# A seven-product (Strassen) step for the second FFN matrix of an encoder kernel

## The chip, the cores and the metric

The kernel runs on one core of one Trainium2 chip. The metric is device time of one execution in microseconds (us), taken as the median of several executions; beside it stands one execution that the hardware profiler recorded. The engines are TensorE (PE in the profile, its weight loads PEld), VectorE (DVE), ScalarE (ACT), GpSimd (POOL) and SyncE (SP), which here only issues DMAs. Every engine takes its own list of instructions in order; an instruction whose operand is not there holds back all that stand behind it.

## The reference

Two layers, each with a mixing block and a SwiGLU block. What matters here is the SwiGLU block (S = 1024 rows, D = 1024, D_FF = 2816, all float32):

```python
h = _rmsnorm(x, g_pre_ffn[l])
gate, up = jnp.split(h @ w_ffn_in[l], 2, axis=-1)
f = (jax.nn.silu(gate) * up) @ w_ffn_out[l]
x = x + _rmsnorm(f, g_post_ffn[l])
```

`act = silu(gate) * up` is a matrix of 2816 x 1024 as the kernel holds it (columns of D_FF on the partitions, rows of the sequence along them), and the second product is `act.T @ w_ffn_out`.

## The kernel before

**Precision.** float32 operands are split into a high part of the faster fp32r format and a low part, what is left of it (`split`, lines 149 to 152: ScalarE casts the high part, VectorE or GpSimd subtracts it, lines 151 and 152). A product of two split matrices takes three matmuls, high by high, high by low and low by high.

**w_ffn_in.** `ffn_in` goes over 11 pairs of 128-column blocks. For each pair two `Quad`s (gate and up) do a seven-product step: sums of blocks of the weights (L1069) and of h (`Blocks`), seven products of 12 matmuls of 128x512 each (L1079), and sums that give the four blocks of the result, s2, z, y and s1 (`snap`, L1084; L1099 to L1115). `gate_out` applies silu, `up_out` multiplies (L1130) and writes two rows of blocks of act to DRAM (`actd`, L1134).

**w_ffn_out.** `ffn_out(l, actd, t0, n, out)` is called three times in a layer, for 3, 3 and 2 tiles of 128 rows. Each call goes over all 22 blocks ff of D_FF: `load_act` reads a block of act for its tiles, `load_ffn_out` the whole block of 128x1024 weights, both are split, and each tile takes 2 halves of the 1024 columns by 3 matmuls (L1179), into two PSUM banks per tile. The last two blocks are done tile by tile (`late = 2`), and `out` gets a tile when it is complete, copied from PSUM by ScalarE and VectorE (L1192, L1193).

**What `out` does.** `last_tile` loads the tile of x (L1306) into one of two slots (`xs_`). In layer 1 `residual_out` squares the tile (L310), computes the scale on GpSimd (L208, L210), multiplies it by scale and gain (L314), adds it to x (L315; GpSimd for tiles 1, 3 and 5) and stores two halves, one from SP and one from ScalarE's queue (L316). In layer 0 `residual` and `norm_x` do the same (L322 to L325) and the first norm of layer 1 (L284, L289), and `norm_T` transposes the tile (L301, target hTp) for layer 1's first matmuls (`zf`, target zT; `kvz`, target kvp).

**What sets the order.** The program is written in the order of the Python code, and a scheduler then places the instructions of each engine; the order within an engine is fixed before the kernel runs. Buffers are slots of two arenas, handed out by rings (`Ring`, `run(first, count, step)`); a slot is taken again when its last reader is done. Four more buffers of 8 KB a partition are called `big`. PSUM tags (`pd`, `av`, `sc`, `pT`) have two banks each. In layer 0 `mem.make()`, keys and values of the memory for layer 1 (targets mTp, kmp, vmp), stands ahead of the first `ffn_out`, and `zf_load` and `fourier_tables` stand between the second and the third.

Of the kernel before, what the change touches and what calls it, by code (L numbers as in the profile page):

```python
# [68 lines left out]
def tile_encoder(ctx: ExitStack, tc: tile.TileContext, T, C, out):  # L69
# [60 lines left out]
    qws, sns, silus, acts = Ring(32, 0, 16, 20), Ring(36, 38, 40, 42, 32, 34), run(8, 5, 2), run(18, 3, 4)  # L130
    sums, wsums = run(8, 4, 2), Ring(4, 6)
    wqs, ars, fs, xs_ = run(44, 3, 4), run(56, 2, 2), run(24, 3, 4), run(36, 2, 4)
# [3 lines left out]
    wcs, wos, ahs = Ring(112, 116, 96, 100, 48, 52, 56, 60), run(80, 6, 4), run(104, 3, 3)  # L136
# [255 lines left out]
    class Memory:  # L392
# [12 lines left out]

        def norm(self, mt):
# [3 lines left out]
            h = at(self.kx + 4 + 4 * mt, D)  # L410
            nc.sync.dma_start(h, T["mem"][0, mt * P : (mt + 1) * P, :])
# [27 lines left out]
        def make(self):  # L439
            self.load_k()  # L440
# [685 lines left out]
    def up_out(q, g, actd, p):  # L1126
        for i, c in enumerate(q.out):
            if i % 2 == 0:
                a = acts(S)
            (nc.gpsimd if i in (0, 3) else nc.vector).tensor_tensor(  # L1130
                out=a[:, 512 * (i % 2) : 512 * (i % 2) + 512], in0=c, in1=g[i], op=ALU.mult
            )
            if i % 2:
                nc.sync.dma_start(actd[2 * p + i // 2], a)  # L1134
# [20 lines left out]
    def load_ffn_out(l, ff):  # L1155
        hi, lo = wos(D, dt=F32R), wos(D, dt=F32R)
        raw = wqs(D)
        nc.sync.dma_start(raw, T["w_ffn_out"][l, ff * P : (ff + 1) * P])
        split(hi, lo, raw)
        return hi, lo  # L1160

    def load_act(actd, ff, t0, n):

        raw = ars(n * P)
        nc.sync.dma_start(raw, actd[ff, :, t0 * P : (t0 + n) * P])
        a = ahs(2, n * P, dt=F32R)
        split(a[:, 0], a[:, 1], raw)
        return a

    def ffn_out(l, actd, t0, n, out):  # L1170

        pts = [[ps([512], "fo", ("pd", "av", "sc")[t]) for _ in range(2)] for t in range(n)]

        def step(ff, t, a, w):
            sl = slice(t * P, t * P + P)
            for m in range(2):
                ns = slice(m * 512, m * 512 + 512)
                for j, (x, y) in enumerate(((0, 0), (0, 1), (1, 0))):
                    mm(pts[t][m], a[:, x, sl], w[y][:, ns], start=ff == 0 and j == 0, stop=ff == NFF - 1 and j == 2)  # L1179

        late = 2
        ops = {}
        for ff in range(NFF):
            ops[ff] = load_act(actd, ff, t0, n), load_ffn_out(l, ff)
            if ff < NFF - late:
                for t in range(n):
                    step(ff, t, *ops[ff])
        for t in range(n):
            for ff in range(NFF - late, NFF):
                step(ff, t, *ops[ff])  # L1190
            f = fs(D)
            nc.scalar.copy(f[:, 0:512], pts[t][0])  # L1192
            nc.vector.tensor_copy(f[:, 512:1024], pts[t][1])  # L1193
            out(t0 + t, f)
# [8 lines left out]
    actd = drp.tile([NFF, P, S], F32, name="actd")  # L1203
# [33 lines left out]
    for l in range(DEPTH):  # L1237
# [57 lines left out]
        if l + 1 < DEPTH:  # L1295
            mem = Memory(l + 1, 16, 0, 24, 36, "pT")
            mix = Mix(l + 1, nhT, mem)
            mem.make()

        def last_tile(t, f):  # L1300
# [9 lines left out]
            residual(x, f, st["gpf"])  # L1310
            st[t] = norm_x(x, st["gpn"], f)
            nc.sync.dma_start(x2d[t], x)
            if t:
                norm_T(st.pop(t - 1), nhT, t - 1, "pT")
# [53 lines left out]
```

## Time and profile before

| | |
|---|---|
| median of 3 executions | 2183.88 us (2183.79 to 2185.25) |
| the profiled execution's own time | 2182.96 us |
| span of its trace | 2181.2 us |
| busy: TensorE, VectorE, ScalarE, GpSimd | 95%, 68%, 50%, 29% |
| mean granted TensorE clock | 0.973 |
| read from HBM, written | 201.76 MB, 49.28 MB |
| w_ffn_out of layer 0, first matmul | at 845.0 us |
| w_ffn_out of layer 1, first matmul | at 1922.8 us |

The span runs from the first to the last recorded instruction. A row of the profile's timeline has the start in us, the length in us, the engine, the line of the kernel, the operation with target and source, and the count of instructions that are merged in it; in square brackets stand idle time ahead of it and what ended that. Rows of groups have busy time, mean time of one in ns, and idle time with what ended it. Busy times of TensorE overlap, since a matmul starts before the one ahead has ended.

### The profile page before, as it was taken

Reading aid. Unit: us, or ns where it says so; the run is one execution under the profiler, and the core shown is the slowest. Engines: PE = TensorE matmul, PEld = TensorE weight load, DVE = VectorE, ACT = ScalarE, POOL = GpSimd, SP = SyncE. Lnnn points to the kernel's source line nnn. Section 1 sums busy time; section 2 is a strip of 40 time slices with the busy share of each in tenths; the row PEclk is TensorE's granted clock in tenths of the full one; section 3 lists DMA queues with packets and bytes.
Section 4 is the critical chain, followed back from the end, with each engine's and each line's share of the span. In section 5 each row is a group of like instructions: output and inputs, shape, how many; then the busy total and the mean of one; then the engine's idle time right before and its main releaser. Section 6 shows DMA issues by size and latency. Waiting matters only on the chain.

```text
span 2181.2 us, 27953 instructions
## 1 busy us (share of the span) xinstructions
PE 2063.6 (95%) x9666; PEld 1708.7 (78%) x9666; DVE 1490.9 (68%) x2352; ACT 1083.4 (50%) x2221; POOL 626.0 (29%) x723
## 2 busy tenths in 40 slices
PE   6998998799999999999999979986999999999997
PEld 6886877588888887888888758775888888888876
DVE  7569767987777765464756686788877767644555
ACT  6467767553333334453545676675433333334343
POOL 4244436532222223010214334465222212100010
PEclk9999999799999999999999989997999999999999
DMA  7112223412223236565721122133222222255765
GB/s 224 37 49 63 73 83 116 135 62 84 87 68 97 78 100 228 195 229 179 239 86 51 35 73 103 53 127 105 74 91 78 97 78 81 92 188 169 245 206 179
DMA packets 135582, 252.87 MB, mean 116 GB/s; under 512 B 11256, under 2 KB 86032, under 8 KB 135440
## 3 DMA queue, kind: packets, MB, share of 16 engines
q1 hardware_dynamic: 127376, 232.20, 32.7%
q10 hardware_dynamic: 8064, 18.88, 2.2%
q8 instruction: 76, 1.25, 0.2%
q14 instruction: 66, 0.54, 0.1%
HBM read 201.76 MB, written 49.28 MB: 115 GB/s over the span
## 4 chain that ended last, share of the span: by engine, by line
PE 82%; DVE 7%; ACT 4%; DMA 3%; issue 2%; POOL 1%; SPq 0%; DVEq 0%; ACTq 0%; POOLq 0%
PE fo L1179 21%; PE qy L1079 11%; PE qz L1079 11%; PE qx L1079 11%; PE mo L162 7%; PE qw L1079 5%; PE qp L162 3%; PE kvp L162 3%; DVE arena_r L152 2%; PE av L767 2%; PE pT L760 2%; PE zT L162 1%; PE sc L723 1%; ACT arena_r L151 1%; DMA arena_f<-in_w_mem_kv 1%
## 5 line engine op out<-in xcount | busy, mean ns | idle before, releaser
L151 ACT CAST arena_r<-arena_f 128x512 fp32r<-128x512 f32 (+4 forms) x736 | 456.4, 640 | 749.3 <-PE fo L1179 170.2
L152 DVE TENSOR_TENSOR arena_r<-arena_f,arena_r 128x512 fp32r<-128x512 f32 (+3 forms) x632 | 515.0, 824 | 338.4 <-ACT arena_r L151 314.7
L1179 PE MATMUL fo<-arena_r 128*128 128x512 f32 x2112 | 490.5, 393 | 9.6 <-ACT arena_r L151 7.6
L1179 PEld LDWEIGHTS fo<-arena_r 128*128 128x128 f32 x2112 | 397.5, 189 | 95.0 <-ACT arena_r L151 9.3
L1079 PE MATMUL qy<-arena_r 128*128 128x512 f32 x1056 | 264.6, 400 | 26.9 <-ACT arena_r L151 24.9
L1079 PEld LDWEIGHTS qy<-arena_r 128*128 128x128 f32 x1056 | 203.3, 194 | 71.7 <-ACT arena_r L151 26.4
L1069 DVE TENSOR_TENSOR arena_f<-arena_f 128x512 f32<-128x512 f32 x220 | 222.2, 1013 | 12.4 <-DMA arena_f<-in_w_ffn_in 7.4
L1079 PE MATMUL qz<-arena_r 128*128 128x512 f32 x704 | 195.9, 389 | 0.0
L1099 POOL TENSOR_TENSOR arena_f<-arena_f 128x512 f32<-128x512 f32 x44 | 64.8, 1473 | 347.6 <-ACT arena_f L1084 347.6
L1079 PEld LDWEIGHTS qz<-arena_r 128*128 128x128 f32 x704 | 132.1, 188 | 27.7 <-DVE arena_r L152 0.3
L208 POOL TENSOR_SCALAR rrsv<-rss 128x1 f32<-128x1 f32 x32 | 11.9, 373 | 425.4 <-ACT arena_f L310 214.8
L1079 PE MATMUL qx<-arena_r 128*128 128x512 f32 x528 | 127.8, 389 | 0.0
L1079 PE MATMUL qw<-arena_r 128*128 128x512 f32 x528 | 127.5, 389 | 0.0
L152 POOL TENSOR_TENSOR arena_r<-arena_f,arena_r 128x256 fp32r<-128x256 f32 (+2 forms) x104 | 85.1, 824 | 146.9 <-ACT arena_r L151 129.1
L1079 PE MATMUL qx<-big,arena_r 128*128 128x512 f32 x528 | 127.1, 389 | 0.0
L1130 POOL TENSOR_TENSOR arena_f<-arena_f 128x512 f32<-128x512 f32 x44 | 72.0, 1636 | 188.9 <-DVE arena_f L1111 128.8
L1079 PE MATMUL qz<-big,arena_r 128*128 128x512 f32 x352 | 115.7, 389 | 0.0
L1079 PEld LDWEIGHTS qx<-arena_r 128*128 128x128 f32 x528 | 99.1, 188 | 20.5
L1079 PEld LDWEIGHTS qx<-big,arena_r 128*128 128x128 f32 x528 | 99.1, 188 | 20.5
L1079 PEld LDWEIGHTS qw<-arena_r 128*128 128x128 f32 x528 | 99.1, 188 | 20.5
L162 PE MATMUL mo<-arena_r 128*128 128x512 f32 x384 | 103.9, 414 | 5.0 <-ACT arena_r L151 4.6
L162 PE MATMUL mo<-big,arena_r 128*128 128x512 f32 x384 | 103.8, 409 | 2.7 <-ACT arena_r L151 1.4
(196 smaller groups left out, 3297.9 us busy)
## 6 DMA issues: line engine op xcount, KB each, us to landing
arena_f<-in_w_ffn_out SPq DMA_DIRECT2D x132, 512.0 KB, 3.6
arena_f<-in_w_ffn_in SPq DMA_DIRECT2D x88, 512.0 KB, 3.6
actd<-arena_f SPq DMA_DIRECT2D x44, 512.0 KB, 4.6
arena_f<-actd SPq DMA_DIRECT2D x88, 192.0 KB, 2.6
arena_f<-in_w_in SPq DMA_DIRECT2D x40, 256.0 KB, 2.9
arena_f<-in_x SPq DMA_DIRECT2D x16, 512.0 KB, 4.4
arena_f<-in_w_out SPq DMA_DIRECT2D x32, 256.0 KB, 2.6
pmd<-arena_f ACTq DMA_DIRECT2D x32, 256.0 KB, 2.0
```

Source lines behind the costliest of these rows:

```text
L151: nc.scalar.copy(hi, src)
L152: return (lo_eng or nc.vector).tensor_tensor(out=lo, in0=src, in1=f32(hi), op=ALU.subtract)
L162: mm(self.dst, a, b, start=self.i == 0, stop=self.i == self.n - 1)
L208: nc.gpsimd.tensor_scalar(out=v, in0=ss, scalar1=1.0 / n, scalar2=EPS, op0=ALU.mult, op1=ALU.add)
L723: mm(pt, lhs, self.kst[g][i][:, k0 * P : k1 * P], start=i == 0, stop=i == 1)
L760: nc.tensor.transpose(pT[:, h, :], es_[h // 2][:, h % 2, j * P : j * P + P], ident)
L767: mm(av, lhs, p_, start=j == 0 and i == 0, stop=j == nk - 1 and i == 1)
L1069: nc.vector.tensor_tensor(out=s, in0=a, in1=b, op=op)
L1079: mm(pt, a, b, start=start and n == 0, stop=n == 11, skip_group_check=not start)
L1099: nc.gpsimd.tensor_tensor(out=self.v, in0=self.v, in1=self.s2, op=ALU.add)
L1130: (nc.gpsimd if i in (0, 3) else nc.vector).tensor_tensor(out=a[:, 512 * (i % 2) : 512 * (i % 2) + 512], in0=c, in1=g[i], op=ALU.mult)
L1179: mm(pts[t][m], a[:, x, sl], w[y][:, ns], start=ff == 0 and j == 0, stop=ff == NFF - 1 and j == 2)
```

## The change

In `ffn_out` all 8 tiles of rows are taken at once as a 2 x 2 block scheme: act has blocks of 512 rows by the even or odd block of each pair in D_FF, the weights the same pairs by halves of the columns. Seven products i = 2, 4, 5, 3, 1, 7, 6 each go over 11 pairs k (a step): one operand of act (128x512) against one of the weights (128x512), for 4 tiles of 128 rows, by 3 matmuls. Products 4, 3 and 7 go on in the PSUM banks of 2, 5 and 1.

- `up_out` makes the seven operands of act in the w_ffn_in stage, three sums and two differences more per pair, on VectorE and GpSimd, and writes each to DRAM, in seven writes of 256 KB where there were two of 512 KB.
- `out_sums` loads one operand of act and one block of the weights (products 2 and 5) or two (the other five), adds or subtracts these (VectorE in even steps, GpSimd in odd ones), and splits both operands. Loads are of 256 KB.
- The sums of the products are kept in the four `big` buffers: copies by ScalarE, sums from PSUM by VectorE, and one difference by GpSimd (L1238) per tile.
- In layer 0 `mem.make()` comes behind product 2, `zf_load` and `fourier_tables` behind product 7; the rows of mem are loaded ahead of the memory's weights, in both layers. `residual` adds on GpSimd but for the last tile. Tiles 0 to 3 are put out within product 6, tiles 4 to 7 behind it.
- In layer 1 (`late`) product 6 is done tile by tile, and tiles 4 to 7 are put out one after the other. Finished operands have 15 slots in layer 1 and 6 in layer 0 (`abs_`), raw ones 3 for act (`ras`) and 6 for the weights (`rbs`).

```diff
-    wqs, ars, fs, xs_ = run(44, 3, 4), run(56, 2, 2), run(24, 3, 4), run(36, 2, 4)
+    ras, rbs, bsums, xs_ = run(40, 3, 2), run(46, 6, 2), Ring(58, 32, 34), Ring(36, 24)
...
     def up_out(q, g, actd, p):
+        V, G = nc.vector, nc.gpsimd
+        a = [acts(512) for _ in range(4)]
         for i, c in enumerate(q.out):
...
+            (G if i in (0, 3) else V).tensor_tensor(out=a[i], in0=c, in1=g[i], op=ALU.mult)
+        a11, a21, a12, a22 = a
...
+        put(3, a11)
+        put(4, a22)
+        for i, x, y, eng in ((1, a11, a22, G), (2, a21, a22, V), (5, a11, a12, G)):
+            s = acts(512)
+            eng.tensor_tensor(out=s, in0=x, in1=y, op=ALU.add)
+            put(i, s)
+        V.tensor_tensor(out=a21, in0=a21, in1=a11, op=ALU.subtract)
+        put(6, a21)
+        G.tensor_tensor(out=a12, in0=a12, in1=a22, op=ALU.subtract)
+        put(7, a12)
...
+    def out_sums(l, actd, i, k):
+        ab = abs_(2, 2, 512, dt=F32R)
+        raw = ras(512)
+        nc.sync.dma_start(raw, actd[i - 1, k])
+        split(ab[:, 0, 0], ab[:, 0, 1], raw)
...
+        if i in (2, 5):
+            s = block(i == 5, i == 5)
+        else:
...
+            x, y = block(*x), block(*y)
+            s = bsums(512)
+            (nc.vector, nc.gpsimd)[k % 2].tensor_tensor(out=s, in0=x, in1=y, op=op)
+        split(ab[:, 1, 0], ab[:, 1, 1], s)
+        return ab
...
+        for i in (2, 4, 5, 3, 1, 7, 6):
+            new = i in (2, 5, 1, 6)
+            if new:
+                pts = [ps([512], "fo", ("pd", "av", "sc", "pT")[p]) for p in range(4)]
+            ops = []
+            for k in range(n):
+                ops.append(out_sums(l, actd, i, k))
+                if i < 6 or i == 7 or not late:
+                    for p in range(4):
+                        step(pts[p], p, ops[k], k == 0, k == n - 1, new)
+                if i == 6 and k in (0, 2, 4, 6):
+                    t = (0, 2, 4, 6).index(k)
+                    out(t, fb[t][:, 0])
...
+                if i == 6 and late:
+                    out(4 + p, fb[p][:, 1])
+            after(i)
...
-            residual(x, f, st["gpf"])
+            residual(x, f, st["gpf"], nc.gpsimd if t < NT - 1 else None)
```

The scheduler's lists at three places, before and now.

SP at the entry of w_ffn_out in layer 0, before: loads of the weights of w_ffn_out, writes and reads of act, and the memory's weights.

```order
L339 DMA arena_f<-in_w_mem_kv 128x4x128 x3
L1158 DMA arena_f<-in_w_ffn_out 128x1024 x2
L339 DMA arena_f<-in_w_mem_kv 128x2x256
L339 DMA arena_f<-in_w_mem_kv 128x4x128
L339 DMA arena_f<-in_w_mem_kv 128x2x256 x2
L1158 DMA arena_f<-in_w_ffn_out 128x1024 x2
```

The same place now; the first read of act (L1178) is step 0's, the second step 1's, the third step 2's.

```order
L1178 DMA arena_f<-actd 128x512
L1140 DMA actd<-arena_f 128x512 x2
L1184 DMA arena_f<-in_w_ffn_out 128x512
L1140 DMA actd<-arena_f 128x512 x4
L339 DMA arena_f<-in_w_mem_kv 128x4x128
L1140 DMA actd<-arena_f 128x512
L339 DMA arena_f<-in_w_mem_kv 128x4x128 x2
L1184 DMA arena_f<-in_w_ffn_out 128x512 x2
L1365 DMA arena_f<-x1d 128x1024
L1178 DMA arena_f<-actd 128x512
L1184 DMA arena_f<-in_w_ffn_out 128x512
L339 DMA arena_f<-in_w_mem_kv 128x2x256
```

The memory's weights no longer stand ahead of the stage's loads but among them, and several stand between step 1's read of act and step 2's.

TensorE at the end of layer 0, before: the last matmuls of w_ffn_out (fo), zT and kvp of layer 1, transposes of the last two tiles (hTp).

```order
L1179 MATMUL fo_8336<-arena_r 128x512 x2
L1179 MATMUL fo_8337<-arena_r 128x512 x2
L162 MATMUL zT_8814<-arena_r 128x512 x6
L162 MATMUL zT_8841<-arena_r 128x512 x23
L162 MATMUL kvp_9020<-big_8986,arena_r 128x512 x6
```

The same place now; hTp_8685 and the five behind it are tiles 1 to 3, hTp_8902 is tile 4.

```order
L1212 MATMUL fo_8517<-arena_r 128x512 x3
L301 MATMUL hTp_8685<-const,big_6977 128x128 x4
L301 MATMUL hTp_8692<-const,big_6977 128x128 x4
L301 MATMUL hTp_8756<-const,big_6978 128x128 x4
L301 MATMUL hTp_8763<-const,big_6978 128x128 x4
L301 MATMUL hTp_8871<-const,big_6979 128x128 x4
L301 MATMUL hTp_8878<-const,big_6979 128x128 x4
L162 MATMUL zT_8916<-arena_r 128x512
L162 MATMUL zT_8943<-arena_r 128x512
L162 MATMUL zT_8916<-arena_r 128x512 x11
L162 MATMUL zT_8943<-arena_r 128x512 x7
```

Transposes of three tiles have moved behind the last product and ahead of zT. VectorE's list there has the sums of tiles 4 to 7 (L1243), gains of tiles 4 to 7 (L324) and the splits of these transposes (L152), now:

```order
L1243 TENSOR_TENSOR big_6979<-fo_8517,big_6979 128x512
L324 SCALAR_TENSOR_TENSOR big_6976<-big_6976,rrs_8859,arena_f 128x1024
L152 TENSOR_TENSOR arena_r<-hTp_8685,arena_r 128x4x128
L324 SCALAR_TENSOR_TENSOR big_6977<-big_6977,rrs_8890,arena_f 128x1024
L152 TENSOR_TENSOR arena_r<-hTp_8692,arena_r 128x4x128
L152 TENSOR_TENSOR arena_r<-hTp_8756,arena_r 128x4x128
L152 TENSOR_TENSOR arena_r<-hTp_8763,arena_r 128x4x128
L152 TENSOR_TENSOR arena_r<-hTp_8871,arena_r 128x4x128
L324 SCALAR_TENSOR_TENSOR big_6978<-big_6978,rrs_9007,arena_f 128x1024
```

The residuals of tiles 4 and 5 now stand among the splits that zT needs.

VectorE at the end of layer 1, before: copies of the last two tiles (L1193), gains (L314) and additions to x (L315).

```order
L1193 COPY arena_f<-fo_16268 128x512
L1193 COPY arena_f<-fo_16270 128x512
L314 SCALAR_TENSOR_TENSOR arena_f<-arena_f,rrs_16662 128x512 x2
L315 TENSOR_TENSOR arena_f<-arena_f 128x512
L314 SCALAR_TENSOR_TENSOR arena_f<-arena_f,rrs_16689 128x512 x2
L315 TENSOR_TENSOR arena_f<-arena_f 128x512 x3
```

The same place now; L1243 is the sum from PSUM of tiles 5, 6 and 7, big_15396 to big_15399 hold tiles 4 to 7, and L315 with big_15398 is tile 2 first and tile 6 later.

```order
L315 TENSOR_TENSOR arena_f<-arena_f,big_15398 128x512 x2
L314 SCALAR_TENSOR_TENSOR big_15396<-big_15396,rrs_16904,arena_f 128x512
L1243 TENSOR_TENSOR big_15397<-fo_16721,big_15397 128x512
L314 SCALAR_TENSOR_TENSOR big_15397<-big_15397,rrs_16951,arena_f 128x512 x2
L315 TENSOR_TENSOR arena_f<-arena_f,big_15396 128x512 x2
L1243 TENSOR_TENSOR big_15398<-fo_16722,big_15398 128x512
L314 SCALAR_TENSOR_TENSOR big_15398<-big_15398,rrs_16998,arena_f 128x512 x2
L315 TENSOR_TENSOR arena_f<-arena_f,big_15398 128x512 x2
L1243 TENSOR_TENSOR big_15399<-fo_16723,big_15399 128x512
L314 SCALAR_TENSOR_TENSOR big_15399<-big_15399,rrs_17045,arena_f 128x512 x2
L315 TENSOR_TENSOR arena_f<-arena_f,big_15399 128x512 x2
```

The sum of tile 7 now stands behind the addition of tile 6, that of tile 6 behind tile 4's, and that of tile 5 behind tile 2's.

More of the change, by code (lines that the diff above doesn't have):

```diff
@@ L404, in load_v, with rows @@
             self.wv = load_w(self.w, MW, MW, self.kw + 16)
+        def rows(self):
+            self.h = [at(self.kx + 4 + 4 * mt, D) for mt in range(2)]
+            for mt in range(2):
+                nc.sync.dma_start(self.h[mt], T["mem"][0, mt * P : (mt + 1) * P, :])
         def norm(self, mt):
@@ L439, in make @@
         def make(self):
+            self.rows()
             self.load_k()
@@ L1170, in ffn_out, with block @@
[L1170 to L1194, printed above, removed]
+    def out_sums(l, actd, i, k):
[3 more added lines that the diff above has]
+        split(ab[:, 0, 0], ab[:, 0, 1], raw)
+        def block(r, c):
+            w = rbs(512)
+            r0 = (2 * k + r) * P
+            nc.sync.dma_start(w, T["w_ffn_out"][l, r0 : r0 + P, c * 512 : c * 512 + 512])
+            return w
+        if i in (2, 5):
+            s = block(i == 5, i == 5)
+        else:
+            x, y, op = {
+                4: ((1, 0), (0, 0), ALU.subtract), 3: ((0, 1), (1, 1), ALU.subtract), 1: ((0, 0), (1, 1), ALU.add),
+                7: ((1, 0), (1, 1), ALU.add), 6: ((0, 0), (0, 1), ALU.add),
+            }[i]
+            x, y = block(*x), block(*y)
[3 more added lines that the diff above has]
+        return ab
@@ L1202, in tile_encoder @@
     kvd = drp.tile([DEPTH, P, 1024], F32, name="kvd")
-    actd = drp.tile([NFF, P, S], F32, name="actd")
+    actd = drp.tile([7, NFF // 2, P, 512], F32, name="actd")
     hT = [None, None]
@@ L1313, in last_tile, with after @@
             if t:
-                norm_T(st.pop(t - 1), nhT, t - 1, "pT")
-        ffn_out(l, actd, 0, 3, last_tile)
-        ffn_out(l, actd, 3, 3, last_tile)
-        if l + 1 < DEPTH:
-            mix.zf_load()
-            mix.fourier_tables(40)
-        ffn_out(l, actd, 6, 2, last_tile)
-        if l + 1 < DEPTH:
-            norm_T(st.pop(NT - 1), nhT, NT - 1, "pT")
-            mix.zf(0)
+                norm_T(st.pop(t - 1), nhT, t - 1, "av")
+        last = l + 1 == DEPTH
+        abs_.i = 0
+        abs_.ks = (64, 72, 80, 88, 16, 24, 0, 8, 32, 40, 48, 56, 96, 104, 112) if last else (80, 88, 48, 56, 96, 104)
+        def after(i):
+            if last:
+                return
+            if i == 2:
+                mem.make()
+            if i == 7:
+                mix.zf_load()
+                mix.fourier_tables(28)
+        ffn_out(l, actd, last_tile, last, after, lambda: mix.zf(0))
+        if not last:
+            norm_T(st.pop(NT - 1), nhT, NT - 1, "av")
 _INS = ['x', 'mem', 'positions', 'g_pre_mix', 'w_in', 'w_fourier', 'sink', 'g_mem', 'w_mem_kv',
```

66 lines of the change are left out of this document (41 added, 25 removed).

## The prediction

> **What bounds the kernel now.** I read the page first: span, engines, chain.
>
> ```profile
> span 2181.2 us, 27953 instructions
> PE 2063.6 (95%) x9666; PEld 1708.7 (78%) x9666; DVE 1490.9 (68%) x2352; ACT 1083.4 (50%) x2221; POOL 626.0 (29%) x723
> PE 82%; DVE 7%; ACT 4%; DMA 3%; issue 2%; POOL 1%; SPq 0%; DVEq 0%; ACTq 0%; POOLq 0%
> L1179 PE MATMUL fo<-arena_r 128*128 128x512 f32 x2112 | 490.5, 393 | 9.6 <-ACT arena_r L151 7.6
> ```
>
> TensorE is the bound: 95% busy, 82% of the chain. The stage that changes is one line, L1179, with 2112 matmuls and 9.6 us of idle time ahead of them. A mean of 393 ns is no pitch, since matmuls overlap; that comes from the TensorE timeline of layer 1.
>
> ```profile
> 1922.81 186.03 PE L1179 MATMUL fo<-arena_r 128*128 128x512 f32 x820
> 2109.41 3.04 PE L1179 MATMUL fo<-arena_r 128*128 128x512 f32 x12 [0.57 <-DVE arena_r L152]
> 2113.41 10.27 PE L1179 MATMUL fo<-arena_r 128*128 128x512 f32 x44 [0.97 <-DVE arena_r L152]
> 2126.09 7.32 PE L1179 MATMUL fo<-arena_r 128*128 128x512 f32 x24 [2.41 <-ACT arena_r L151]
> 2134.85 35.66 PE L1179 MATMUL fo<-arena_r 128*128 128x512 f32 x156 [1.44 <-ACT arena_r L151]
> ```
>
> 186.03 us for 820 matmuls are 226.9 ns each, unbroken. The same pitch holds in the w_ffn_in stage, by the stage windows (columns: window, length, busy us and count of PE, PEld, DVE, ACT, POOL, clock, DMA share, GB/s):
>
> ```profile
> 460.00:820.00 360.00, 360.00 (x1590) 298.20 (x1589) 257.68 (x324) 133.71 (x231) 83.81 (x59) 1.00 0.27 88
> 870.00:1060.00 190.00, 189.63 (x906) 158.98 (x905) 107.81 (x123) 89.30 (x137) 25.42 (x25) 1.00 0.61 201
> 2050.00:2100.00 50.00, 50.00 (x222) 41.44 (x221) 21.96 (x26) 18.87 (x27) 0.00 (x0) 1.00 0.56 178
> ```
>
> In all three TensorE never waits at clock 1.00, VectorE has 28% or more to spare, and the DMA engines 39% or more. So a matmul less is 226.9 ns less, as long as the others keep up.
>
> **The change, part by part.**
>
> *Matmuls removed.* Per layer 22 x 8 x 2 x 3 = 1056 become 7 products x 11 steps x 4 tiles x 3 = 924. Twice 132 are 264, by 226.9 ns: **-59.9 us**.
>
> *Waits at the end of layer 1.* From 1922.81 to 2134.85 + 35.66 = 2170.51 are 247.7 us; 1056 x 0.2269 are 239.6. The 8.1 us of waits and slow clock come where one pass of tiles follows another. The change has no such passes, and the list of VectorE below has every split of the last product ahead of the output of tile 0. I leave 1 us for new places: **-7.1**.
>
> *Operands of a step.* A step is 12 matmuls, 12 x 0.2269 = 2.72 us. VectorE makes two low halves for it, and in 5 of 7 products every second step an addition; POOL makes the other addition. The two engines do not run freely beside each other (timelines of VectorE, then of POOL):
>
> ```profile
> 565.54 0.69 DVE L152 TENSOR_TENSOR arena_r<-arena_f,arena_r 128x512 fp32r<-128x512 f32 x1 [2.04 <-ACT arena_r L151]
> 566.27 1.67 DVE L1069 TENSOR_TENSOR arena_f<-arena_f 128x512 f32<-128x512 f32 x1
> ```
>
> ```profile
> 566.08 1.31 POOL L1099 TENSOR_TENSOR arena_f<-arena_f 128x512 f32<-128x512 f32 x1 [15.02 <-ACT arena_f L1084]
> ```
>
> Alone 0.69 us, beside a POOL addition 1.67: it ends when POOL has ended plus its own time. A POOL addition thus takes about 1.0 us from VectorE. Two steps of a two-block product: 4 low halves and one addition, 5 x 0.69 = 3.45; POOL 1.0; the product's four sums from PSUM, 4 x 0.69 over 11 steps, 0.5. Together 4.95 of 5.44 us: a cover of 0.25 us per step, thin. ACT has 2 x 0.62 of 2.72. DMA by the packets of a stretch with only 2 KB rows, and the landing of such a load:
>
> ```profile
> q1 hardware_dynamic: 1152, 2.10, 12.6%
> arena_f<-in_w_in SPq DMA_DIRECT2D x5, 256.0 KB, 2.7
> ```
>
> The stretch is 55 us: 0.126 x 16 x 55 / 1152 = 96 ns a packet. A two-block step has 3 x 128 packets, 384 x 96 / 16 = 2.31 of 2.72 us. It fits again, 85% full. Two thin covers in 110 steps: between 0 and 31 us lost (a pitch of 3.0), I take **+3**, near the rows.
>
> The Trainium skill, page "SBUF — State Buffer", section "The DMA setup-cost knee", says that a transfer pays about 2 us however small, and puts one of 256 KiB at 224 GB/s; by that figure 786 KB of a two-block step would take 3.5 us, and 110 steps lose 87 us. The trace of a crowded stretch (2022 to 2046 us, loads of 192 and 512 KB) speaks against taking loads one by one:
>
> ```profile
> DMA packets 3221, 8.25 MB, mean 344 GB/s; under 512 B 363, under 2 KB 1365, under 8 KB 3218
> arena_f<-actd SPq DMA_DIRECT2D x8, 192.0 KB, 5.6
> ```
>
> Overlapping loads reached 344 GB/s, but a load then took 5.6 us to land.
>
> *w_ffn_in stage.* Per pair of blocks VectorE gets two instructions (2 x 0.69) and POOL three (3 x 1.0 taken from VectorE), 4.4 us in 14 products of 2.72, 38 us; VectorE goes from 72% to 83%. TensorE covers it: 0. If the cover failed it would cost at most the 22 x 4.4 us.
>
> *Entry, layer 0.* The next layer's memory moves from ahead of the stage to behind product 2. Its matmuls stay (96 and 16 transposes), and so do its eight weight loads, its splits, and the four loads and POOL splits of zf; on SP they now stand between the loads of product 2 (list in the change). Now TensorE waits once and is slow afterwards:
>
> ```profile
> 845.02 12.71 PE L1179 MATMUL fo<-arena_r 128*128 128x512 f32 x54
> 861.53 10.87 PE L1179 MATMUL fo<-arena_r 128*128 128x512 f32 x36 [3.79 <-ACT arena_r L151]
> ```
>
> 3.8 idle, then 36 matmuls in 10.87 instead of 8.2: 6.5 us. After, the load of step 1 goes into slot 42, which holds s2 of the last quad until POOL has multiplied it, and on SP all later loads stand behind it; the memory's weights, before ahead, are mixed in. I take 4 us idle and 2 slow: **0** net, from -6 to +6. In layer 1 the third step has that slot, one step later: nothing.
>
> The Trainium skill, "TensorE: Matmul & The Clock Gate", section "What's actually happening", halves the clock after an idle window of about 3.4 us. The rows show the slow stretch after 3.79 us, but a smaller one after 2.41 us too (24 in 7.32 us, not 5.45); by the page alone the waits that I price under its window would come without their slow stretch, some 2 us less in the sum.
>
> *Exit, layer 0.* Before, TensorE passes from the last pass into work that lay ready:
>
> ```profile
> 1114.42 1.98 PE L1179 MATMUL fo<-arena_r 128*128 128x512 f32 x8
> 1116.23 6.74 PE L162 MATMUL zT<-arena_r 128*128 128x512 f32 x29
> ```
>
> After, four tiles end at once, and the transposes of tiles 1 to 3 stand between the last product and zT (list in the change). Their PSUM tag has two banks, so each waits for splits on VectorE, which has residuals of tiles 4 and 5 between them. From the last matmul, T: sum of tile 4 at T-1.3, square 1.25, POOL 0.85, so its gain at 0.8; gain 1.28, split 0.69, gain of tile 5 1.28, four splits 2.8: zT can start at about T+6.9. Transposes fill 2.4 of it. 4.5 idle and 2.5 slow: 7. The sums of the tiles fill the four big buffers, so the weights of kvp, which lay ready before, come only as tiles 4 to 7 are transposed; pq and the second half of zT stand between, and I count nothing for it. In the last product itself POOL adds rows of 1024, which hold VectorE for some 2 us each, four times:
>
> ```profile
> L325 POOL TENSOR_TENSOR arena_f<-arena_f x14: 2349/2391/3427, 326.6 to 1480.0; 128x1024 f32<-128x1024 f32 x14
> L289 DVE SCALAR_TENSOR_TENSOR arena_f<-arena_f,nrs 128x1024 f32<-128x1024 f32 x7 | 9.0, 1282 | 2.0 <-POOL nrs L210 1.9
> ```
>
> VectorE then has 22 x 0.69 + 10 x 0.69 + 8 x 1.28 + 8 + 5 = 45 us for 30, of which six steps (some 13) lie ahead in the ring: 2 us late. Together **+9**, from 0 to 18.
>
> *Tail.* Now 10.7 us, from 2170.51 to 2181.2. After, all eight tiles go out within the last product, through two x slots (arena 36 and 24): a slot is loaded again when both halves of its tile are stored. VectorE and POOL take the tiles in order, so tile 7's sum stands behind tile 6's addition. The prices are stores L316 and loads L1306 to landing (min/median/max, a row each); the third row, of the chain, is a store that already held back an x load before:
>
> ```profile
> DMA to landing us min/median/max: 2.0/2.8/7.2
> DMA to landing us min/median/max: 3.8/5.2/8.6
> 2110.93 6.08 DMA out<-arena_f
> ```
>
> From the end of product 7: tile 0 stored at about 7.5; x2 loaded at 11.5, added by 13.4, stored 16; x4 at 20, added 21.4; SP issues x6 only after tile 5's store (25, POOL), so x6 lands at 29 and is added by 30.6. Then sum, square, power, two gains, addition 5.5, store and end 3.3: 39.4, against 26.3 for the matmuls left. A tail of 13.1 with loads of 4.0; 3.6 more with 5.2. **+4.5**, from -1 to +10.
>
> *Start.* Rows of mem load earlier, one transpose of them stands ahead of the first zT: 0, give or take 2.
>
> Sum: -59.9 - 7.1 + 3 + 0 + 9 + 4.5 + 0 = **-50.5**. From the profiled execution, 2182.96 (span 2181.2 and 1.8 around it), 2132.5. The median is 0.9 higher: **2133.5 us**.
>
> **Rivals.** *Supply becomes the bound in the two-block products.* For: 91% and 85% full, VectorE in order, SP in order, three raw slots for act. Against: rings of 6 and 15 finished operands, and the one-block products 2 and 5 build a lead. At a pitch of 2.9 to 3.1 in 110 steps: +20 to +42 less the 3 counted: 2150 to 2172.
>
> *Slower: the act slots.* One raw slot of three is held for landing, ACT 0.62, VectorE 0.69 and about 0.7 of queueing. At 2.7 us landing that is 4.7 / 3 = 1.6 us a step; at 5.6 still 2.5. At the 8.6 of the slowest load above it is 3.5: 110 x 0.8 = 88 us, 2218. It decides from 7.5 us of landing on (pitch 3.17, which eats 50 us). The crowded stretch shows 5.6, so it is unlikely. The Trainium skill's 224 GB/s would end on the same side.
>
> *No loss at the seams.* Exit, tail and supply at nothing: 2183.9 - 67 = 2117, and less with the entry's 6.5. For: before's exit shows none. Against: the lists.
>
> *The change not doing what it says* is out: TensorE's list has 924 products a layer.
>
> **How the numbers follow.** Forecast, 2118 to 2150: 0.64. No loss at the seams, 2110 to 2118: 0.09. Supply, 2150 to 2172: 0.16. Within 0.2% of 2183.9, which is about what a measurement of this kernel can tell from no change: 0.04, supply at a pitch near 3.2. Slower: 0.07. Faster by over 0.2% is the rest, 0.89. The range 2112 to 2166 leaves out the last two and the outer parts of two rivals, 0.2.
>
> **What would show it.** TensorE in layer 1 from the first product to the last matmul near 924 x 0.2269 = 209.7 us, at clock 1.00; 2 to 4 us of idle time at layer 0's second or third step; idle time ahead of the first zT after layer 0, released by VectorE's splits; in the tail, waits for DMA x1d on VectorE and POOL, and 13 to 16 us after the last matmul. Idle time ahead of L1212 in products 4, 3, 1, 7 with VectorE near 95% or the DMA share over 0.9 would make the supply right and my forecast too low. VectorE at 0.69 beside POOL's additions would make my lock wrong.

## The result and the profile after

| | before | changed |
|---|---|---|
| median of 4 executions | 2184.14 us (2183.79 to 2185.25) | 2162.33 us (2151.62 to 2168.58) |
| ratio to before | | 0.9894 [0.9854, 0.9935] |
| profiled execution, span | 2182.96, 2181.2 us | 2151.62, 2149.5 us |

The change makes the kernel 1.1% faster, clear of the interval, where 2.3% was forecast. The time lies inside the range, but the gain is less than half of the forecast. The profiled execution is the fastest of the four, so the rows below show a gain of 31.7 us in span and not the median's 21.8. Of the 28.7 us that the median lacks of the forecast's 50.5, these rows can account for 18.8; the other 9.9 lie between this execution and the median.

The page of the changed kernel, the same lines that were shown of before: span, busy time of the engines, chain by engine, and TensorE's line of w_ffn_out, now L1212.

```profile
span 2149.5 us, 28257 instructions
PE 2007.0 (93%) x9402; PEld 1662.2 (77%) x9402; DVE 1625.6 (76%) x2517; ACT 1070.4 (50%) x2273; POOL 846.9 (39%) x854
PE 73%; DVE 8%; DMA 7%; POOL 4%; ACT 4%; issue 3%; SPq 0%; POOLq 0%; ACTq 0%; DVEq 0%
L1212 PE MATMUL fo<-arena_r 128*128 128x512 f32 x1848 | 430.9, 395 | 15.2 <-ACT arena_r L151 12.3
```

264 matmuls are gone (x2112 became x1848), and the idle time ahead of that line rose from 9.6 to 15.2 us. In the chain TensorE lost nine points, to DMA and GpSimd above all. That says where to look, but it is no price: nine points of the span are far more than what is missing. TensorE's timeline of w_ffn_out in layer 1 has it in four rows, where before had 820 matmuls in a single unbroken one.

```profile
1911.11 5.60 PE L1212 MATMUL fo<-arena_r 128*128 128x512 f32 x24
1921.10 86.41 PE L1212 MATMUL fo<-arena_r 128*128 128x512 f32 x372 [4.39 <-ACT arena_r L151]
2011.51 0.49 PE L1212 MATMUL fo<-arena_r 128*128 128x512 f32 x1 [4.00 <-ACT arena_r L151]
2012.32 121.38 PE L1212 MATMUL fo<-arena_r 128*128 128x512 f32 x527 [0.31 <-DVE arena_r L152]
```

924 matmuls at 226.9 ns are 209.7 us; from 1911.11 to 2012.32 + 121.38 = 2133.70 they take 222.6. Of the 12.9 us between, 8.7 are idle in three rows, and 3.8 are slow clock behind the waits (372 in 86.41 instead of 84.4, 527 in 121.38 instead of 119.6). The waits fall on two steps, the third and the 34th, and on no other.

**The third step.** ScalarE, GpSimd and SyncE around 1916 us, from their timelines:

```profile
1920.43 0.62 ACT L151 CAST arena_r<-arena_f 128x512 fp32r<-128x512 f32 x1 [2.51 <-DMA arena_f<-actd]
```

```profile
1913.72 1.29 POOL L1196 TENSOR_TENSOR arena_f<-arena_f 128x512 f32<-128x512 f32 x1 [10.73 <-DMA arena_f<-in_w_ffn_out]
1914.98 1.74 POOL L1136 TENSOR_TENSOR arena_f<-arena_f 128x512 f32<-128x512 f32 x1
```

```profile
1916.75 0.33 SPq L1178 DMA_DIRECT2D arena_f<-actd  x1
```

Read backwards: TensorE starts at 1921.10 when the cast of its operand ends; the cast waited for a load of act; SyncE issued that load at 1916.75, when GpSimd's multiplication L1136 had freed slot 42; and that multiplication stood behind an addition L1196, which had waited for a block of weights. It is the held slot that the prediction described for layer 0 and ruled out for layer 1.

**The 34th step.** TensorE's list there, layer 1 (names with 15830 to 15833 are the PSUM banks of products 5 and 3, 16268 to 16271 those of products 1 and 7):

```
L1212 MATMUL fo_1433_15833<-arena_r_72 128x512 x3
L1212 MATMUL fo_1434_16268<-arena_r_72 128x512 x3
L1212 MATMUL fo_1435_16269<-arena_r_72 128x512 x3
L1212 MATMUL fo_1436_16270<-arena_r_72 128x512 x3
L1212 MATMUL fo_1437_16271<-arena_r_72 128x512 x3
L1212 MATMUL fo_1434_16268<-arena_r_72 128x512 x3
L1212 MATMUL fo_1435_16269<-arena_r_72 128x512
L1212 MATMUL fo_1430_15830<-arena_r_72 128x512 x5
```

Product 3 goes on in the banks of product 5, so it must wait until these are read; such a place is called a seam below. The scheduler put 16 matmuls of product 1 in between. Their operands are made 11 steps later than those of product 3, so TensorE waited for a load of act while the operands of product 3 lay ready. Here the lead counts, which is the number of steps by which the reads of act (L1178) are ahead of TensorE. When it began to wait, at 2007.5 us, it had done 33 steps and SyncE had issued 46 reads, the last of them 0.9 us before: a lead of 13 was not enough. The cast that ended the wait, and the reads issued by then:

```profile
2010.32 2.79 ACT L151 CAST arena_r<-arena_f 128x512 fp32r<-128x512 f32 x5 [3.34 <-DMA arena_f<-actd]
```

```profile
L1178 SPq DMA_DIRECT2D arena_f<-actd x46: 319/327/1004, 1871.8 to 2006.6; - x46
```

Layer 0's timeline of TensorE has the same seam as a plain wait for the sum (960.21), the entry's wait (853.44), and the exit (1088.82, 1095.64):

```profile
853.44 27.57 PE L1212 MATMUL fo<-arena_r 128*128 128x512 f32 x108 [3.48 <-ACT arena_r L151]
960.21 61.71 PE L1212 MATMUL fo<-arena_r 128*128 128x512 f32 x264 [2.44 <-DVE big L1237]
1088.82 1.97 PE L301 MATMUL hTp<-const,big 128*128 128x128 f32 x16 [2.87 <-DVE big L1243]
1095.64 9.20 PE L162 MATMUL zT<-arena_r 128*128 128x512 f32 x26 [4.85 <-ACT arena_r L151]
```

The stretches of the two profiled executions, by TensorE's rows (target qp, the queries of layer 1, is the first work that the exit no longer disturbs; its rows have the first and last start in us):

```profile
L162 PE MATMUL qp<-big,arena_r x384: 387/389/502, 129.8 to 1257.3; 128*128 128x512 f32 x192
```

```profile
L162 PE MATMUL qp<-big,arena_r x384: 387/389/633, 128.7 to 1246.3; 128*128 128x512 f32 x192
```

| stretch | before | changed | difference | forecast |
|---|---|---|---|---|
| start to w_ffn_out, layer 0 | 845.0 | 847.1 | +2.1 | 0 |
| from there to the last qp | 412.3 | 399.2 | -13.1 | -19.5 |
| from there to w_ffn_out, layer 1 | 665.5 | 664.8 | -0.7 | 0 |
| w_ffn_out, layer 1 | 247.7 | 222.6 | -25.1 | -35.5 |
| last matmul to the end | 10.7 | 15.8 | +5.1 | +4.5 |
| sum | | | -31.7 | -50.5 |

### The profile page after: what moved, and what is told of

Its sections match the earlier page's. It is cut to its first block, busy times and chain, and to the rows that moved or that the text cites. A ratio compares the mean times of both kernels' runs of the same rounds, so it can differ in the third digit from the quotient of the medians.

```text
span 2149.5 us, 28257 instructions
## 1 busy us (share of the span) xinstructions
PE 2007.0 (93%) x9402; PEld 1662.2 (77%) x9402; DVE 1625.6 (76%) x2517; ACT 1070.4 (50%) x2273; POOL 846.9 (39%) x854
## 4 chain that ended last, share of the span: by engine, by line
PE 73%; DVE 8%; DMA 7%; POOL 4%; ACT 4%; issue 3%; SPq 0%; POOLq 0%; ACTq 0%; DVEq 0%
PE fo L1212 12%; PE qz L1084 11%; PE qy L1084 11%; PE qx L1084 11%; PE mo L162 6%; PE qw L1084 5%; PE kvp L162 4%; PE qp L162 3%; DVE arena_r L152 3%; DMA arena_f<-actd 2%; PE sc L728 2%; PE av L772 2%; PE pT L765 1%; ACT arena_r L151 1%; DMA arena_f<-in_w_ffn_out 1%
## 5 line engine op out<-in xcount | busy, mean ns | idle before, releaser
L151 ACT CAST arena_r<-arena_f 128x512 fp32r<-128x512 f32 (+1 forms) x780 | 443.7, 591 | 689.6 <-PE qz L1084 117.2
L152 DVE TENSOR_TENSOR arena_r<-arena_f,arena_r 128x512 fp32r<-128x512 f32 (+1 forms) x676 | 539.4, 821 | 178.5 <-ACT arena_r L151 175.0
L1212 PE MATMUL fo<-arena_r 128*128 128x512 f32 x1848 | 430.9, 395 | 15.2 <-ACT arena_r L151 12.3
L1212 PEld LDWEIGHTS fo<-arena_r 128*128 128x128 f32 x1848 | 350.9, 191 | 91.7 <-ACT arena_r L151 14.8
L1074 DVE TENSOR_TENSOR arena_f<-arena_f 128x512 f32<-128x512 f32 x220 | 210.0, 958 | 8.2 <-DMA arena_f<-in_w_ffn_in 3.2
L1104 POOL TENSOR_TENSOR arena_f<-arena_f 128x512 f32<-128x512 f32 x44 | 70.1, 1593 | 305.8 <-ACT arena_f L1089 305.8
L1196 POOL TENSOR_TENSOR arena_f<-arena_f 128x512 f32<-128x512 f32 x50 | 74.0, 1481 | 267.2 <-DVE arena_r L152 134.7
L1136 POOL TENSOR_TENSOR arena_f<-arena_f 128x512 f32<-128x512 f32 x44 | 73.5, 1672 | 165.2 <-DVE arena_f L1116 127.3
L152 POOL TENSOR_TENSOR arena_r<-arena_f,arena_r 128x256 fp32r<-128x256 f32 (+2 forms) x104 | 85.5, 826 | 130.9 <-ACT arena_r L151 121.5
```

The costliest lines, as they stand in the source:

```text
L151: nc.scalar.copy(hi, src)
L152: return (lo_eng or nc.vector).tensor_tensor(out=lo, in0=src, in1=f32(hi), op=ALU.subtract)
L1074: nc.vector.tensor_tensor(out=s, in0=a, in1=b, op=op)
L1104: nc.gpsimd.tensor_tensor(out=self.v, in0=self.v, in1=self.s2, op=ALU.add)
L1136: (G if i in (0, 3) else V).tensor_tensor(out=a[i], in0=c, in1=g[i], op=ALU.mult)
L1196: (nc.vector, nc.gpsimd)[k % 2].tensor_tensor(out=s, in0=x, in1=y, op=op)
```

## Experiments

Each kernel is the changed one with the edit shown, unless another is named. The kernels ran in three sets, against medians of before of 2183.8, 2182.2 and 2182.7 us. Every difference below is from the changed kernel's 2158.28 us of the first set, so across sets it is uncertain by the 1 to 2 us by which the medians of before differ.

### The changed kernel again

> The changed kernel once more, nothing altered; it is the measure for the three other runs of this set, and shows how far its executions lie apart (so far 2151.6 to 2168.6 us, where the kernel before spans 1.5 us). Theory A (the waits that TensorE has at a few fixed places of w_ffn_out end with the landing of a DMA, so their length varies from one execution to the next): median 2156 to 2166, a spread of 10 us or more, and the same places idle in this trace (layer 0: step k=1 and the start of product 3; layer 1: step k=2 and the start of product 1), by different amounts. Theory B (the spread was that of one chip): within 3 us of one value.

2158.28 us (2156.09 to 2159.81), ratio 0.9884 [0.9869, 0.99]: the measure for the others. The spread is 4 us here, the waits are at the same four places. In layer 1 they are longer:

```profile
1918.15 5.60 PE L1212 MATMUL fo<-arena_r 128*128 128x512 f32 x24
1928.37 86.65 PE L1212 MATMUL fo<-arena_r 128*128 128x512 f32 x372 [4.62 <-ACT arena_r L151]
2020.15 122.23 PE L1212 MATMUL fo<-arena_r 128*128 128x512 f32 x528 [5.13 <-ACT arena_r L151]
```

224.2 us for the stage. What spread the first set over 17 us stays open; of the 8 us between the two profiled executions this stage has 1.6, and the stretches ahead of it the rest. This execution, 2159.81 us, is nearer to the median than the first, and the stretches of its trace against before and the forecast are: start +4.4 (0), from there to the last qp -11.5 (-19.5), to w_ffn_out of layer 1 +2.4 (0), w_ffn_out of layer 1 -23.5 (-35.5), tail +4.6 (+4.5). So 20 of the 27 us that it lacks are lost in the two w_ffn_out stages with the exit.

### Slots 32 and 42 exchanged

```diff
-    ras, rbs, bsums, xs_ = run(40, 3, 2), run(46, 6, 2), Ring(58, 32, 34), Ring(36, 24)
+    ras, rbs, bsums, xs_ = Ring(40, 32, 44), run(46, 6, 2), Ring(58, 42, 34), Ring(36, 24)
```

> One pair of buffers exchanged: slot 42 (s2 of the last quad, held until GpSimd has multiplied it) goes from the act loads to the third use of the sums of weights, slot 32 (free early) to the act loads. Theory A (head of line at the entry: the load into slot 42 waits for GpSimd's multiplication): the waits of 3.5 us at layer 0's step k=1 and of 4.4 us at layer 1's step k=2 go with their slow clock, 8 to 13 us faster than the changed kernel in the same set. Theory B (the operands are late there anyway, since loads, splits and sums of the first steps stand behind the work of the w_ffn_in stage): TensorE waits a step or two later for about as long, and the time moves by less than 3 us.

2156.92 us, 1.4 below: theory B by the time, but not by its reason. The wait at the third step is gone (132 matmuls of product 2 unbroken), and another stands at the next seam. TensorE, then ScalarE:

```profile
1921.40 30.08 PE L1212 MATMUL fo<-arena_r 128*128 128x512 f32 x132
1957.93 66.17 PE L1212 MATMUL fo<-arena_r 128*128 128x512 f32 x280 [6.45 <-ACT big L1233]
```

```profile
1954.38 1.20 ACT L151 CAST arena_r<-arena_f 128x512 fp32r<-128x512 f32 x2 [2.10 <-POOL arena_f L1196]
1955.73 1.66 ACT L151 CAST arena_r<-arena_f 128x512 fp32r<-128x512 f32 x3 [0.16 <-POOL arena_f L1196]
1957.30 1.06 ACT L1233 COPY big<-fo 128x512 f32<-128x512 f32 x2
```

Product 4 goes on in the banks of product 2 and needs their copy; the copy stands in ScalarE's list behind casts whose sums of weights GpSimd had just made. The slot was the cause of its wait, but the operands had no lead yet, and the next place that asked for one paid.

### The order of the products

```diff
-        for i in (2, 4, 5, 3, 1, 7, 6):
+        for i in (2, 5, 4, 3, 1, 7, 6):
```

> Products in the order 2, 5, 4, 3, 1, 7, 6, so that 4 and 3 do not come right behind the product in whose PSUM banks they go on (sums arranged to suit; the memory of layer 1 comes behind product 4, one product later). TensorE's list then has no 16 matmuls of product 1 ahead of product 3 in layer 1. Theory A (those 16 matmuls were put ahead by the scheduler to fill the wait for the sums, but their operands are made 11 steps later, so TensorE waited 4.0 us for them; in layer 0 it waited 2.4 us for the sum itself): both waits go with their slow clock, 6 to 10 us faster than the changed kernel. Theory B (supply has run dry there): a wait of 2 to 4 us stays near the 33rd step, and the time moves by less than 3 us.

2143.21 us, 15.1 below, more than either theory. Both waits of theory A went: TensorE in layer 1 passes the 34th step inside one row, at 226.9 ns but for 1.9 us of slow clock at its head.

```profile
1918.02 144.65 PE L1212 MATMUL fo<-arena_r 128*128 128x512 f32 x629 [1.80 <-DVE arena_r L152]
```

w_ffn_out of layer 1 takes 219.4 us (224.2), and layer 0's, from first to last matmul, 234.4 (237.7): theory A by the places. The third step still waits (2.44 and 1.80 us), and the seam that this order keeps, product 7 right behind product 1, has three small waits (1.6 us in all). But in layer 0 the last qp comes no sooner behind the first matmul (400.7 us, 400.8), so those 3 us are lost again at the exit, and 12 us come from a stretch that the edit doesn't touch, from the last qp to w_ffn_out of layer 1: 655.7 us where the unaltered one has 667.9. The scheduler makes the order of the whole program anew: of the 2883 matmuls and transposes that TensorE does there, 815 stand at another place. Its idle time in the stretch is 34.8 us instead of 41.5 and its mean granted clock 0.97 instead of 0.96. Where the order is the unaltered one (the changed kernel's two executions, seven x slots below) the stretch took 664.8 to 668 us. Another order need not be faster: with the additions on VectorE, further below, 803 stand elsewhere and it took 667.6.

### Seven x slots in layer 1

```diff
+        if last:
+            xs_.i, xs_.ks = 0, (36, 24, 28, 20, 16, 12, 0)
```

> Layer 1 alone: seven slots for x in the tail in place of two, all else as in the changed kernel. Theory A (the chain of two slots, load behind store, sets the tail): from the last matmul to the end 15.8 us becomes 10 to 12, 4 to 6 us faster. Theory B (VectorE and GpSimd in order set it: sums, squares, gains, additions): 14 to 16 us stay, less than 1.5 us faster.

2152.23 us, 6.1 below; theory A, and a little more. The last matmul ends at 2027.10 + 117.97 = 2145.07, the span at 2154.3: a tail of 9.2 us in place of 15.3.

```profile
2027.10 117.97 PE L1212 MATMUL fo<-arena_r 128*128 128x512 f32 x512 [1.82 <-DVE big L1237]
```

### The rows of mem, in the changed kernel and in the one before

```diff
-            self.rows()
```

> The changed kernel with one part undone: the rows of mem are loaded where the kernel before loads them, behind the memory's weights. Theory A (the earlier rows put transposes ahead of the first zT and turn the scheduler's order in the mixing stage of layer 0; that is the 2 to 7 us by which w_ffn_out of layer 0 starts later than before): its first matmul comes back to 845 to 846 us, and the time is 2 to 6 us below the changed kernel's 2158. Theory B (other causes, or chance of the execution): it stays at 847 to 852, and the time within 2 us.

2150.48 us, 7.8 below, more than either theory and not where theory A has it: w_ffn_out of layer 0 starts at 847.2, as late as in the changed kernel; the gain is in layer 1's mixing (last qp to w_ffn_out 657.7 us, with 827 matmuls at another place). The counterpart puts the rows early in the kernel before:

> The kernel before with one part of the change alone: the rows of mem are loaded ahead of the memory's weights, in both layers. Theory A (this edit, through the order that the scheduler then makes of the mixing stages, costs in itself; undoing it in the changed kernel gave 8 us): 3 to 9 us slower than the kernel before, in the stretches ahead of w_ffn_out in layer 0 (845.0) or of layer 1 (1922.8), with w_ffn_out itself as before. Theory B (the order of the mixing stages falls out by chance with any edit): within 3 us, or faster.

2180.64 us (2178.03 to 2186.0, 10 executions), ratio 0.9986 [0.9976, 0.9996]: theory B. The first matmul of w_ffn_out came 6 us later (851.0), and the rest of the program gave it back and 2 us more. The edit has no cost of its own there; it turns the order of the mixing stages, either way.

### Three and four edits together

> Three edits tried alone before, together: slots 32 and 42 exchanged, the order of products 2, 5, 4, 3, 1, 7, 6, seven x slots in layer 1. Theory A (the exchange of slots moved TensorE's wait to the place where product 4 waits for the copies of product 2, since those copies stand on ScalarE behind casts that wait for loads; with the other order that place is gone): w_ffn_out of layer 1 takes 212 to 217 us from first to last matmul (224.2 in the changed kernel, 219.4 with the order alone), the tail 9 to 10, and the time is 2130 to 2137. Theory B (the wait moves on once more): 219 us or more, 2137 to 2143.

2132.26 us, 0.9766 [0.9746, 0.9785]: the time of theory A; w_ffn_out of layer 1 takes 218.4 us, between the theories, the tail 9.3. What is left in the stage are a wait of 1.89 us with its slow clock, and four small ones (2.2 us in all) at the seam to product 7.

> Slots 32 and 42 exchanged, products in the order 2, 5, 4, 3, 1, 7, 6, seven x slots in layer 1 (2132.3 together) and the rows of mem loaded late as in the kernel before. Theory A (the rows cost 8 us by themselves): 2122 to 2127. Theory B (they only turned the order of layer 1's mixing stage, which the new order of products has already turned back: 758.7 us from the exit's pq to w_ffn_out of layer 1, against 768.6): 2128 to 2134.

2132.70 us: theory B. With the new order of products the rows bring nothing.

### Four x slots in layer 0

```diff
+        xs_.ks = (36, 24) if last else (36, 24, 16, 20, 36, 24, 36, 24)
```

> Layer 0 alone: four slots for x in place of two for tiles 0 to 3 (two again for tiles 4 to 7). In the changed kernel GpSimd waited 4.6 us for the load of x for tile 2, with the norm of tiles 2 and 3 behind it. Theory A (the chain of two x slots, not a full VectorE, delays the transposes at the exit): the idle time ahead of the transposes of tile 2 (2.9 to 4.0 us, ended by VectorE) goes, zT starts 3 to 6 us sooner after the last matmul, the time 3 to 6 us below 2158. Theory B (VectorE's own work sets it): zT still starts 9 to 12 us after the last matmul, the time within 2 us.

2158.11 us: theory B by the time. GpSimd's wait for x at the exit went from 4.6 us to 2.7, yet zT starts 249.7 us behind the first matmul of w_ffn_out (853.2), against 248.5 and 249.4 in the two executions of the changed kernel. The wait ahead of the transposes of tile 2 went, as theory A has it, and zT follows the last matmul after 8.7 us instead of 10.6 and 11.7; but TensorE waits inside product 6 instead (1.66 and 2.88 us, both ended by VectorE, where 1.17 stood), so the last matmul comes later by as much. Behind it TensorE now waits in one place, ended by the casts of the transposes:

```profile
1094.00 2.78 PE L301 MATMUL hTp<-const,big 128*128 128x128 f32 x24
1102.86 8.19 PE L162 MATMUL zT<-arena_r 128*128 128x512 f32 x25 [6.08 <-ACT arena_r L151]
```

### GpSimd's additions on VectorE

```diff
-            (nc.vector, nc.gpsimd)[k % 2].tensor_tensor(out=s, in0=x, in1=y, op=op)
+            nc.vector.tensor_tensor(out=s, in0=x, in1=y, op=op)
...
-                    nc.gpsimd.tensor_tensor(out=c11[p], in0=c21[p], in1=c22[p], op=sub)
+                    TT(out=c11[p], in0=c21[p], in1=c22[p], op=sub)
...
-            residual(x, f, st["gpf"], nc.gpsimd if t < NT - 1 else None)
+            residual(x, f, st["gpf"])
```

> The additions that the w_ffn_out stage has on GpSimd (every second sum of weights, layer 0's residuals, the difference behind product 5) go to VectorE; the w_ffn_in stage stays. Theory A (an addition on GpSimd takes about 1.0 us from VectorE, more than the 0.69 that it costs there; operands have a lead of many steps, so supply is no bound): VectorE is no later, and the time is within 3 us of the changed kernel's 2158, or better where GpSimd's queue held something back. Theory B (VectorE is full, GpSimd's share is needed): TensorE waits for low halves in the two-block products, 10 to 40 us slower.

2153.41 us, 4.9 below: theory A, though 1.6 of that may be the set's. w_ffn_out of layer 1 takes 221.2 us instead of 224.2, and its two waits are shorter, 3.07 and 3.57 us instead of 4.62 and 5.13. The same on top of the four edits:

> The same four edits, and the additions of the w_ffn_out stage on VectorE in place of GpSimd (4 us less by itself). Theory A (that gain was made at the exit of layer 0, which the other edits leave as it is): 2 to 4 us below the four edits. Theory B (it was the order of other stages): within 2 us of the four edits, or above.

2121.97 us (2119.48 to 2122.86), ratio 0.9716 [0.9697, 0.9735]: the best version here, 10.7 below the four edits, more than either theory. The larger part is not the exit: w_ffn_out of layer 1 takes 211.2 us in place of 221.1, one wait of 1.26 us in it, while from the first matmul in layer 0 to the last qp the gain is 2.8 us. (The trace of the four edits is of an execution 5 us above their median; the three edits, with the same stage, took 218.4 us, so the stage gained 7 to 10 us.)

```profile
1898.75 35.54 PE L1212 MATMUL fo<-arena_r 128*128 128x512 f32 x156
1935.55 174.38 PE L1212 MATMUL fo<-arena_r 128*128 128x512 f32 x768 [1.26 <-ACT arena_r L151]
```

Windows of 60 us at the same place in the stage, in both of which TensorE never waits (window, length, busy us and count of PE, PEld, DVE, ACT, POOL, clock, DMA share, GB/s), the four edits first:

```profile
1945.00:2005.00 60.00, 60.00 (x266) 49.69 (x265) 46.47 (x65) 26.93 (x47) 15.79 (x11) 1.00 0.91 316
```

```profile
1939.00:1999.00 60.00, 60.00 (x267) 49.67 (x266) 50.97 (x82) 30.25 (x54) 0.00 (x0) 1.00 0.96 336
```

Once GpSimd adds nothing beside it, VectorE does 17 instructions more in 4.5 us more, on average 622 ns each instead of 715, and more operands are made while TensorE does the same work. The lead shows it: when 55 steps are done, at the seam to product 7, it is 16 steps and TensorE passes without a wait; with the four edits it is 13, and TensorE waits 4.2 us in four pieces, the longest 2.68.

### One block of weights in place of two

```diff
-            x, y = block(*x), block(*y)
-            s = bsums(512)
-            (nc.vector, nc.gpsimd)[k % 2].tensor_tensor(out=s, in0=x, in1=y, op=op)
+            s = block(*x)
```

> The changed kernel with the second block of the weights and its addition left out in products 4, 3, 1, 7 and 6 (their operand is the first block alone), so that those steps load 512 KB in place of 768 and add nothing: 110 loads and 110 additions less. Theory A (supply of operands is no bound in the two-block products; only the waits at the entries and seams are): the stretches of TensorE between those places stay at 226.9 ns a matmul as before, w_ffn_out of layer 1 shortens by 5 us at most (from 224), the whole by 10 at most. Theory B (supply costs a few tenths of a microsecond in each two-block step): 10 to 30 us less.

2143.04 us, 15.2 below; products 4, 3, 1, 7 and 6 lack the second block. w_ffn_out of layer 1 takes 215.7 us, 8.5 less. Neither theory as it stood: the pitch doesn't move (179.82 us for 792 matmuls are 227.0 ns), yet supply counts, since the wait at the 34th step is gone though the 16 matmuls still stand there. Operands that come faster have built the lead by then: when 33 steps are done, 50 reads of act have been issued, a lead of 17. In the changed kernel it is 12 and 13 in its two executions (waits of 5.13 and 4.00 us), and 13 with the additions on VectorE (3.57 us). Whether the loads or the additions that are left out bring this is not separated here.

```profile
1944.39 179.82 PE L1210 MATMUL fo<-arena_r 128*128 128x512 f32 x792 [0.28 <-ACT big L1231]
```

```profile
L1178 SPq DMA_DIRECT2D arena_f<-actd x50: 319/320/425, 1869.2 to 2003.0; - x50
```

## Why the prediction was wrong, step by step

**Matmuls removed (-59.9): right.** 924 a layer at 226.9 ns wherever TensorE doesn't wait (768 in 174.38 us above).

**Waits at the end of layer 1 (-7.1): this step failed.** It said "I leave 1 us for new places", because the change has no passes of tiles. The old places did go, but the change has seams of its own: products 4, 3 and 7 each go on in banks that must first be read. At one of them the scheduler had pulled matmuls forward whose operands were not there yet. Together with the next step 1 + 1.5 us were left in layer 1; 12.9 were lost, 4.39 idle and 2.0 slow at the third step, 4.31 idle and 1.8 slow at the 34th. The order of the products shows the cause of the second wait, the exchange of slots that of the first. In layer 0 the seam at 960.21 costs 2.44 idle and 1.8 slow, not counted either; in the run with the other order it is gone, but the last qp came no sooner, so what would be saved without it is not shown.

**Operands of a step (+3): mechanism half right, sized by the wrong quantity.** The pace holds, as forecast: no row loses time between the waits. It was priced as a pace alone (5.0 of 5.44 us), but a thin cover means that a lead is built slowly, and every place that asks for operands ahead of their turn, or holds a slot, pays until it is there. That supply matters through the lead is shown by one block in place of two (lead of 17 instead of 12 or 13 at the 34th step, no wait, -8.5 us in the stage) and by the additions moved to VectorE (lead of 16 instead of 13 at the seam to product 7, no wait). What sets the pace at which the lead grows was not found: in the 60 us ahead of the 34th step VectorE is busy for 37.07 us (62%) and the DMA share is 0.85, both below the signs that the prediction named. The lock between the two engines was right. Timelines of VectorE and of GpSimd in the changed kernel:

```profile
1914.88 0.69 DVE L152 TENSOR_TENSOR arena_r<-arena_f,arena_r 128x512 fp32r<-128x512 f32 x1 [0.22 <-ACT arena_r L151]
1915.49 1.78 DVE L1196 TENSOR_TENSOR arena_f<-arena_f 128x512 f32<-128x512 f32 x1
```

The addition that takes 1.78 us ran beside GpSimd's L1136 from 1914.98 (shown above). The Trainium skill, "SBUF — State Buffer", section "SBUF: two separate sides", calls the port pair of the two engines an exclusive lock for a VectorE instruction with two SBUF inputs against a GpSimd one that reads SBUF; this trace agrees (1.78 us beside it, 0.69 alone), and the runs show the price.

The rival "supply becomes the bound" named 2150 to 2172, where the median lies, but by a pitch of 2.9 to 3.1 us a step, which no row shows; that the number fits is chance. The rival of the act slots did not occur: it needed loads of act that land after 7.5 us, and their median is 4.2.

**w_ffn_in stage (0): right.** The window of the same place (460 to 820 us; columns as above) has TensorE without a gap and VectorE at 80%, forecast 83%:

```profile
460.00:820.00 360.00, 360.00 (x1590) 298.10 (x1589) 289.44 (x343) 132.01 (x230) 137.97 (x89) 1.00 0.32 107
```

**Entry, layer 0 (0): right, and wrong for layer 1.** Forecast 4 idle and 2 slow; measured 3.48 and 3.1 (108 matmuls in 27.57, not 24.5), against 6.5 before. The sentence "In layer 1 the third step has that slot, one step later: nothing" is falsified: 4.39 idle and 2.0 slow. It trusted in the one step more of time, and left out what stood ahead of the multiplication on GpSimd, an addition that the change itself puts there.

**Exit, layer 0 (+9): mis-sized.** 1.17, 2.87 and 4.85 us idle, and 26 matmuls of zT in 9.20 instead of 5.9: 12.2. The place is as forecast, and VectorE's work ended the first two waits. The longest, ahead of zT, was ended by ScalarE's casts, while the prediction's chain ends with VectorE's splits: zT started 10.6 us behind the last matmul, where that chain gave 6.9. On ScalarE the last two casts stood behind the squares of tiles 4 to 7 and a pass of the next norm (L284) that waited for GpSimd's addition:

```profile
1093.48 1.06 ACT L284 ACTIVATE big<-arena_f 128x1024 f32<-128x1024 f32 x1 [0.42 <-POOL arena_f L325]
1094.53 1.05 ACT L151 CAST arena_r<-hTp 128x512 fp32r<-128x512 f32 x2
```

Neither four x slots nor the additions on VectorE brought zT forward by more than 2 us (249.7 and 247.5 us behind the first matmul). Which item would have to move was not tried by itself.

**Tail (+4.5): right.** A tail of 15.8 us against 15.2 forecast, and the chain of two slots was its cause: with seven slots it was 9.2.

**Start (0 +- 2): the edit costs nothing, the order does.** Rows of mem moved alone cost nothing over the whole of the kernel before. But the same instructions between the last qp and w_ffn_out of layer 1 took 655.7 to 667.9 us in these kernels, by the order that the scheduler happened to make. In the changed kernel's two executions that is -0.7 and +2.4 against before, and the start +2.1 and +4.4. With the rows loaded late the start was still +2.2, so they are not its cause, and that stays open. Such a term belonged into the range on both sides; what in that order decides was not found.

## What to carry to other kernels

Count, beside the work removed, every place where the new scheme makes TensorE ask for something ahead of its turn: banks to be read before the next product goes on in them, a buffer still held by the stage before, an instruction that a scheduler has pulled forward. Supply that is enough by its pace still pays at each of these until a lead is built; so put independent work between products that share banks, and keep additions off an engine that locks out the one that makes the operands. A whole-program scheduler turns stages that an edit doesn't touch, here by up to 12 us, so compare by stages before a cause is named.

## What the runs showed of the hardware

The slow clock came behind shorter waits than the 2.41 us of the rows of before, but not behind every one of them. Behind 1.89 us of idle time the granted clock stood at 0.50 for 3.4 us, and 504 matmuls lost 1.8 us (116.18, not 114.4; three edits together). Behind 2.18 us 264 matmuls lost 0.2 (60.10, not 59.9; four x slots, layer 0), and behind 1.26 us 768 lost nothing (174.38, shown above).

```profile
1942.50 116.18 PE L1212 MATMUL fo<-arena_r 128*128 128x512 f32 x504 [1.89 <-ACT arena_r L151]
```

```profile
965.88 60.10 PE L1212 MATMUL fo<-arena_r 128*128 128x512 f32 x264 [2.18 <-DVE big L1237]
```

Counted over the w_ffn_out stages of all traces here: no wait from 1.0 to 1.66 us had a slow stretch of its own, 8 of the 12 between 1.82 and 2.20 us had one, and so had every one of 2.41 us or more. What decides in between was not found; it may be one way in which two executions of the same kernel come to differ. The Trainium skill, "TensorE: Matmul & The Clock Gate", section "What's actually happening", asks for an idle window of about 3.4 us; here the measurement differs, and a wait of about 2 us should be priced with a slow stretch as likely, though not certain.
